# One core of Trainium2: the meta tokens' attention of a hybrid decoder, taken out of the pairs' pipeline and done for eight heads at once

## The chip, the core and the metric

The kernel runs on one core of one Trainium2 chip. The metric is the device time of one execution in microseconds (us). Before the change it is 1934.89 us, the median of three runs (1934.46 to 1937.74). The core's engines work on their own instruction queues and meet through semaphores: TensorE (PE for its matmuls, PEld for its weight loads), VectorE (DVE), ScalarE (ACT), GpSimd (POOL), and SyncE (SP), whose queue issues the DMAs.

## The reference, cut to what matters

The reference is a trunk of two layers (DEPTH is 2) over 16 learned meta tokens followed by 1024 positions, 1040 rows of width 1024. Each layer normalizes its input and projects it into the operands of two parallel mixers: sliding-window attention, and an mLSTM with four heads. Both outputs are gated and go through one output projection. The first 16 rows are dropped at the end.

```python
h = rms_norm(x, norm_g)
z = h @ w_in
aq, ak, av, ag, mq, mk, mv, mi, mf, mo, mgate = split(z)
q = partial_rope(rms_norm(aq.reshape(B, L, 16, 64), q_norm_g))
k = partial_rope(rms_norm(ak.reshape(B, L, 2, 64), k_norm_g))
ya = sliding_window_sink_attention(q, k, av, sink) * silu(ag)
...
y = concatenate([ya, ym]) @ w_out
return x + y
```

There are 16 query heads and 2 key heads, eight query heads to each key head. A query sees itself and the 127 positions before it, and also all 16 meta tokens; each head has one more logit, its sink, that takes part in the softmax but has no value. A meta token's own query therefore sees only the meta tokens up to itself, and the sink: a 16 by 16 lower triangle and one column. That part of the attention is needed in layer 0 alone, since the meta rows of layer 1's output are dropped.

## The kernel before, in words

All matmuls are in full float32 accuracy by splitting operands into a high and a low float32r part and adding the products. The rows are cut into nine tiles (`TT`): tile 0 has the 16 meta rows, tiles 1 to 8 have 128 rows each. Layer by layer the kernel runs four stages: keys and values for all tiles (`kv_tasks`) and the first group of queries; the attention; the mLSTM; the output projection.

**The attention stage** goes through eight pairs of heads, `j` = 0 to 7 (pairs 0 to 3 use key head 0, pairs 4 to 7 key head 1, `kv`). For each pair it goes through blocks of queries `b` (`att_tasks`). In layer 0 these are nine, b = 0 to 8, block 0 being the meta tokens; in layer 1 `first_q` is 1 and there are eight. A block passes four steps:

- `s1` (L680): the scores of both heads into a score tile S, four matmuls (L692). S is two PSUM banks wide, one bank for each head, and there are two such tiles, used in turn. Then the mask (L704 to L711), the maximum (L715), the exponential (L718), the reciprocal of the sum (L720) and the scaling (L723). Some blocks' S also takes turned queries of a coming pair in its free columns 384 to 511 (`q_turn`, L633, and `q_take`, L639 to L642: the `visits`), and in layer 0 block 6's takes the meta queries of the next pair (`q_meta_turn`, L646).
- `s2`, two blocks later: the probabilities are transposed into the one bank T (L738, L741), and split into high and low parts by ACT and DVE (L745, L746, L748, L749); POOL makes a masked copy, OW (L756).
- `s3`, three blocks later: the first product with the values into the one bank O (L766).
- `s4`, behind s3: the other products (L778) into O. ACT takes half of O out (L781), DVE adds the other half (L783), POOL multiplies the result into the gate tile G (L785), and SP stores finished chunks of G to `spool` in DRAM (L789).

For block 0 the forms are small: 16 queries and 16 keys in s1, one 16x16 transpose in s2, nothing in s3, two products of 16 columns in s4.

**What sets the order.** Beside the attention, projections run: while pair j passes, the gates (even j, `g_tasks`, 22 parts for two pairs) or the next queries (odd j below 7, `q_tasks`, 24 parts in layer 1 and 25 in layer 0, where the meta tile is a part of its own) or the mLSTM's first values (j = 7, 25 parts) are computed in small parts (L234 and, for the meta tile, L218). A q group is taken out of its bank by ACT (L580, L581) and DVE (L584) at its last part. `weave` spreads the items of the pair's steps evenly over the parts:

```python
for i, f in enumerate(fg):
    f()
    upto = (i + 1) * len(bg) // len(fg)
    for g in bg[done:upto]:
        g()
```

`fg` are the parts and `bg` the items: four for each step (s1 of one block, s2 of an earlier one, s3 and s4 of one earlier still), so 36 a pair in layer 0 and 32 in layer 1. In this stage PE's instructions keep exactly this order (`pin`). The order on ACT, DVE and POOL, and PE's in the mLSTM, is set by a scheduler that runs through the program with a simulated time; `high_priority` puts some instructions ahead. Weights come by DMA (L161) and are split by ACT (L167) and POOL (L168) into a ring of buffers; their loads hang on places in the list of parts, their splits on `s2` of certain blocks. The stage ends when the last block has passed s4, and the mLSTM follows with the rest of the projections (L194).

Of the kernel before, what the change touches and what calls it, by code (L numbers as in the profile page):

```python
# [12 lines left out]
F32R = mybir.dt.float32r  # L13
# [10 lines left out]
NEG = -1e30  # L24
# [12 lines left out]
WHEN = {0: (3, 4, 5, 6), 3: (2, 3, 4, 5), 4: (3, 4, 6, 7)}  # L37
FIRST = ((0, 0), (0, 1), (1, 0))


def _tables():
# [10 lines left out]
    cst = np.zeros((128, 166), f)  # L52
    cst[:, 0:128] = np.eye(128, dtype=f)
    cst[:, 128:164] = -0.5
    for r in range(64):
        cst[r, 164 + r // 16 % 2] = 1.0
    return {
# [7 lines left out]
def build(ctx, tc, I, O):  # L65
# [307 lines left out]
    for l in range(DEPTH):  # L373
# [5 lines left out]
        AV = unit(F32R)[:, 0:896].rearrange("p (t c) -> p t c", t=7)  # L379
        DV = unit(F32R)[:, 0:896].rearrange("p (t c) -> p t c", t=7)  # L380
# [3 lines left out]
        KT = unit()[:, :].rearrange("p (a c) -> p a c", a=8)  # L384
        SS = []
# [87 lines left out]
        def kv_tasks():  # L473
# [13 lines left out]
            if l == 0:  # L487
# [4 lines left out]
                sy.dma_start(cst, I["cst"])  # L492
# [25 lines left out]
            for i in range(4):  # L518
                ve.tensor_scalar(VM[:, i // 2, i % 2, :], ident, 0.0, None, ALU.mult)
            for i, t in enumerate(ts):  # L520
# [123 lines left out]
        def q_meta_turn(j, ps):  # L644
            c0 = 128 * (j % 2)
            pin(pe.transpose(ps, A[j]["q"]["XM"][:, c0:c0 + 128], ident[:16, :16]))  # L646

        def q_meta(j, ps):

            q_meta_turn(j, ps)  # L650
            q_put(q_unit(j, 0)[:, 1024:1056], ps, 16)

        def g_tasks(j, wgf, co, st):
            def chunk_parts(c):
# [4 lines left out]
                def finish(ps):  # L659
                    if c == 0:  # L660
                        st["G"] = unit()
                    th = t384(e - a)
                    sc.activation(th, ps[:, :e - a], AF.Tanh, scale=0.5)
                    ve.scalar_tensor_tensor(st["G"][:, a:e], th, 1.0, ps[:, :e - a], ALU.add, ALU.mult)
                return projT_parts(wgf, co, a, e - a, finish)
# [11 lines left out]
        def att_tasks(j, st):  # L677
# [3 lines left out]
            def s1(b):  # L681
# [4 lines left out]
                k0, kn, o = (0, 16, 128) if b == 0 else (0, 144, 128) if b == 1 else (16 + (b - 2) * 144, 272, 0)  # L686
                for h in range(2):
                    U = st["Q", b > 4]
                    i = (b - 1) % 4
                    lq = U[:, 1024 + 16 * h:1040 + 16 * h] if b == 0 else U[:, 512 * h + 128 * i:512 * h + 128 * i + 128]  # L690
# [3 lines left out]
                meta = b == 6 and j < 7 and first_q == 0  # L694
                if meta:
                    q_meta_turn(j + 1, S[:, 0, 384:400])
# [6 lines left out]
                if b == 0:  # L703
                    ve.memset(band[:p], NEG)  # L704
                    mk = mask[:p, 128:144].bitcast(U32).rearrange("p (a c) -> p a c", a=1).to_broadcast([p, 2, 16])
                    ve.copy_predicated(cols(S, 130, 510, 16)[:p], mk,
                                       neg[:p].rearrange("p (a c) -> p a c", a=1).to_broadcast([p, 2, 16]))
                else:
                    if b == 1:
                        ve.memset(cols(S, 2, 510, 128), NEG)  # L710
                    ve.copy_predicated(band, mask.bitcast(U32).rearrange("p (h c) -> p h c", h=2),  # L711
                                       cols(S, 146, 366, 128))
# [13 lines left out]
                if meta:  # L726
                    q_put(q_unit(j + 1, 0)[:, 1024:1056], S[:, 0, 384:400], 16)
                live[b] = P

            def s2(b):  # L730
# [3 lines left out]
                HL = OW = None  # L734
# [4 lines left out]
                if b > 0:  # L739
                    for h in range(2):  # L740
                        pin(pe.transpose(X[:, 128 * h:128 * h + 128], P[:, 1 + 160 * h:129 + 160 * h], ident))  # L741
                with tc.high_priority(offset=EARLY):
                    if b > 0:
                        HL = p512(F32R)
                        sc.activation(HL[:, 0:256], X[:, 0:256], AF.Copy)  # L745
                    taken = sc.activation(pm[0:32, 0:p], tm, AF.Copy).ins  # L746
                    if b > 0:
# [619 lines left out]
```

## Time and profile before

| what | value |
|---|---|
| median of three runs | 1934.89 us (1934.46 to 1937.74) |
| the profiled execution | 1933.47 us |
| its span, first to last instruction | 1931.7 us |
| granted TensorE clock | 1.000 |
| busy over the span: PE, PEld, DVE, ACT, POOL | 98%, 93%, 54%, 55%, 51% |

The profile's page is of one execution. "Idle" of an engine is time with no instruction running on it; the waits view says which instruction came after such a time and which one, as far as semaphores tell, let it go. A row of the timeline has the start in us from the beginning of the span, the length in us, the engine, the line, the operation, what it writes and reads, the shape, and a count where like instructions are merged. A row of the windows view has the stretch, its length, then the busy us of each engine with its number of instructions in brackets, the granted clock, the DMA engines' busy share and GB/s. Matmuls are pipelined: a new one starts before the last has ended, so a group's share of TensorE's time is read from the start of one group to the start of the next.

### The profile page before, as it was taken

To read this page: it belongs to the slowest core of one execution; us is meant where nothing else is said; L and a number is where in the kernel's file an instruction comes from. 1 tells how busy PE (TensorE), PEld (TensorE's weight loads), DVE (VectorE), ACT (ScalarE), POOL (GpSimd) and SP (SyncE) were. 2 spreads that over 40 slices of the span, in tenths; PEclk is the share of its full clock that TensorE was granted. 3 is DMA by queue.
4 is the path that set the end of the run, shared out by engine and by line. 5 is a ranking of instruction groups with operands and counts; after the bars stand their busy time and mean duration, and the time that the engine had idled before them with its cause. 6 is when DMAs were issued, how large, how long until landed. Compare 5 with 4: busy or idle time off the path is not lost.

```text
span 1931.7 us, 36274 instructions
## 1 busy us (share of the span) xinstructions
PE 1902.6 (98%) x12827; PEld 1796.5 (93%) x12827; DVE 1051.2 (54%) x2914; ACT 1065.0 (55%) x3193; POOL 988.7 (51%) x1278
## 2 busy tenths in 40 slices
PE   8999999999999999999999999999999999999999
PEld 7999999999999999977789999999999999998887
DVE  7666766667354453542545667666573635437211
ACT  6577777746454554643334778776564545446221
POOL 3665756346545454564325467564465543647332
PEclk9999999999999999999999999999999999999999
DMA  4111111121222121554541111112122121216543
GB/s 155 32 45 40 38 44 43 45 65 41 64 54 59 43 62 50 154 170 159 176 134 36 44 48 38 49 48 60 40 59 64 47 71 41 62 59 195 167 148 125
DMA packets 150839, 148.28 MB, mean 77 GB/s; under 512 B 15081, under 2 KB 123921, under 8 KB 150658
## 3 DMA queue, kind: packets, MB, share of 16 engines
q1 hardware_dynamic: 150658, 145.97, 25.8%
q8 instruction: 101, 1.65, 0.4%
q14 instruction: 80, 0.66, 0.1%
HBM read 122.58 MB, written 23.29 MB: 76 GB/s over the span
## 4 chain that ended last, share of the span: by engine, by line
PE 82%; DVE 5%; ACT 3%; DMA 3%; POOL 3%; issue 2%; SPq 0%; ACTq 0%; POOLq 0%; DVEq 0%
PE pj L194 32%; PE pj L234 19%; PE pss L1260 6%; PE pj L1260 5%; PE po L1260 4%; PE S L692 3%; PE O L778 3%; PE po L957 2%; PE pss L957 2%; PE O L766 2%; PE T L741 1%; DMA raw<-in_w_out_dram 1%; DVE t L903 1%; PE pt L957 1%; PE pj L218 1%
## 5 line engine op out<-in xcount | busy, mean ns | idle before, releaser
L194 PE MATMUL pj<-H,RING 128*128 128x384 f32 (+2 forms) x3312 | 559.3, 322 | 0.0
L194 PEld LDWEIGHTS pj<-H,RING 128*128 128x128 f32 x3312 | 521.5, 188 | 2.3 <-issue 0.2
L168 POOL TENSOR_TENSOR RING<-raw,RING 128x512 fp32r<-128x512 f32 (+1 forms) x192 | 256.8, 1343 | 107.3 <-ACT RING L167 100.3
L234 PE MATMUL pj<-RING,H 128*128 128x256 f32 (+1 forms) x1920 | 268.8, 286 | 0.0
L234 PEld LDWEIGHTS pj<-RING,H 128*128 128x128 f32 x1920 | 242.2, 189 | 0.5
L234 PE MATMUL pj<-H,RING 128*128 128x384 f32 (+2 forms) x1296 | 239.7, 325 | 0.0
L186 POOL TENSOR_TENSOR RING<-raw,RING 128x512 fp32r<-128x512 f32 x96 | 126.1, 1320 | 172.8 <-ACT RING L185 159.7
L194 PE MATMUL pj<-RING,H 128*128 128x256 f32 x1536 | 209.6, 287 | 4.0 <-DVE w1k L202 2.1
L234 PEld LDWEIGHTS pj<-H,RING 128*128 128x128 f32 x1296 | 200.9, 188 | 0.1
L194 PEld LDWEIGHTS pj<-RING,H 128*128 128x128 f32 x1536 | 193.7, 191 | 6.5 <-DVE w1k L202 2.5
L185 ACT ACTIVATE RING<-raw 128x512 fp32r<-128x512 f32 x128 | 80.6, 631 | 174.8 <-DMA raw<-in_w_out_dram 155.4
L167 ACT ACTIVATE RING<-raw 128x512 fp32r<-128x512 f32 (+1 forms) x196 | 122.2, 625 | 47.0 <-DMA raw<-in_w_in_dram 35.2
L970 POOL TENSOR_TENSOR p<-u,p 128x258 fp32r<-128x258 f32 x64 | 49.5, 774 | 172.9 <-ACT p L969 164.9
L718 ACT ACTIVATE t<-S,mx 128x145 f32<-128x145 f32 (+1 forms) x272 | 99.4, 368 | 43.9 <-DVE mx L715 35.3
L785 POOL TENSOR_TENSOR u<-u,w1k 128x128 f32<-128x128 f32 (+1 forms) x136 | 61.9, 455 | 118.0 <-DVE w1k L783 102.2
L1260 PE MATMUL pss<-RING,H 128*128 128x512 f32 x384 | 120.5, 394 | 0.0
L756 POOL TENSOR_SCALAR_AFFINE_SELECT p<-p 128x512 fp32r<-128x512 f32 x112 | 71.4, 637 | 86.7 <-DVE p L748 85.7
L1260 PE MATMUL pj<-RING,H 128*128 128x512 f32 x352 | 110.3, 395 | 0.0
L903 DVE SCALAR_TENSOR_TENSOR t<-u,cw,t 128x384 f32<-128x384 f32 (+1 forms) x144 | 107.6, 747 | 2.0
L723 ACT ACTIVATE t<-t,mx 128x144 f32<-128x144 f32 (+1 forms) x272 | 97.7, 407 | 7.1 <-DVE mx L720 6.5
L926 DVE SCALAR_TENSOR_TENSOR t<-t,pj 128x384 f32<-128x384 f32 (+2 forms) x48 | 24.5, 511 | 124.9 <-ACT t L925 124.9
L1260 PE MATMUL po<-RING,H 128*128 128x512 f32 x288 | 91.3, 398 | 0.0
(347 smaller groups left out, 3841.3 us busy)
## 6 DMA issues: line engine op xcount, KB each, us to landing
raw<-in_w_out_dram SPq DMA_DIRECT2D x128, 256.0 KB, 2.8
raw<-in_w_in_dram SPq DMA_DIRECT2D x100, 256.0 KB, 2.8
raw<-in_w_in_dram SPq DMA_DIRECT2D x192, 128.0 KB, 2.3
spool<-u SPq DMA_DIRECT2D x56, 192.0 KB, 1.9
p<-x SPq DMA_DIRECT2D x24, 256.0 KB, 4.2
t<-spool SPq DMA_DIRECT2D x30, 192.0 KB, 3.6
p<-spool SPq DMA_DIRECT2D x26, 192.0 KB, 3.6
u<-em SPq DMA_DIRECT2D x8, 576.0 KB, 6.6
```

The source lines that it names most:

```text
L167: sc.activation(hi, raw[:, :, 0:o], AF.Copy)
L168: eng.tensor_tensor(lo, raw[:, :, 0:o], hi, op=ALU.subtract)
L185: sc.activation(hi, raw, AF.Copy)
L186: (ve if i > 8 and i % 2 else gp).tensor_tensor(lo, raw, hi, op=ALU.subtract)
L194: last = pin(pe.matmul(out, a, b, start=(i == 0), stop=(i == n - 1)))
L234: pin(pe.matmul(out(), x, y, start=(k + i == 0), stop=(k == n - 1 and i == 2)))
L718: sc.activation(P[:p, 145 * h:145 * h + 145], S[:p, h, 1 + 127 * h:146 + 127 * h], AF.Exp, bias=mx[:p, 0, h:h + 1], accum_out=mx[:p, 1, h: ...
L723: sc.activation(Pn, Pn, AF.Copy, scale=mx[:p, 2, h:h + 1])
L756: gp.affine_select(OW, HL, [[0, 4], [1, 128]], ALU.is_ge, 0.0, base=0, channel_multiplier=-1)
L903: ve.scalar_tensor_tensor(z, RAW[:, t0 + i:t0 + i + n], wcol(i), z, ALU.mult, ALU.add)
L957: pin(f(*a, **k))
L1260: pin(pe.matmul(ps[:p, :], a, b, start=(i + n == 0), stop=(i == 15 and n == len(terms) - 1)))
```

## The change

Block 0 goes out of the pairs' pipeline. Every pair has eight blocks in both layers, b = 1 to 8, and 32 items in its weave. In layer 0 the meta queries are handled so instead:

- After each of the four query groups, the turned meta queries of four heads are split and put into one stationary operand `QM`, which has eight heads by 16 meta queries, 128 columns, for each key head. It lies in free columns of the unit that holds `AV`. The first group is put there before the attention, the others in block 6 of pairs 1, 3 and 5 (before: one pair at a time, eight times).
- Two blocks carry the rest (`MRIDE`): block 4 of pair 3 for key head 0, block 4 of pair 7 for key head 1. Their s1 has two more matmuls, into columns 384 to 399 of S's first bank: 128 rows (eight heads by 16 queries) by 16 meta keys. `meta_probs` masks, adds the sink column and takes the softmax. Their s2 has one more transpose, into T's free columns, and its split into `pmm`, which lies in free columns of the unit that holds `DV`. Their s4 has one more product of 128 columns, into O's columns 256 to 383, and `meta_out` takes it out of the bank, adds the halves, multiplies with the gates and stores the 16 meta rows of four pairs to `spool`.
- The gates' first 16 columns are copied by POOL into `GM` (free space of VR's first tile) as each gate chunk 0 is done; nine small DMAs in pair 0 bring the triangle and the sinks into free space of KR's first tile.
- The store of a pair's first chunk begins at column 16 in both layers.

```diff
+MRIDE = ((3, 4), (7, 4))
...
+        def q_meta_turn(m, ps):
+            for i in range(2):
+                pin(pe.transpose(ps[:, i], QQ[m]["XM"][:, 128 * i:128 * i + 128], ident[:16, :16]))
...
+        def meta_probs(S, kv):
+
+            X = S[:, 0, 384:401]
+            one = lambda x: x.rearrange("p (a c) -> p a c", a=1)
+            ve.copy_predicated(one(X[:, 0:16]), one(mcst[:, 32:48].bitcast(U32)), one(neg).to_broadcast([128, 1, 16]))
+            ve.tensor_copy(X[:, 16:17], mcst[:, 48 + kv:49 + kv])
+            P, mx = mcst[:, 0:17], mcst[:, 20:23]
+            ve.tensor_reduce(mx[:, 0:1], X, axis=mybir.AxisListType.X, op=ALU.max, negate=True)
+            sc.activation(P, X, AF.Exp, bias=mx[:, 0:1], accum_out=mx[:, 1:2])
+            ve.reciprocal(mx[:, 2:3], mx[:, 1:2])
+            sc.activation(P[:, 0:16], P[:, 0:16], AF.Copy, scale=mx[:, 2:3])
+            return P
+
+        def meta_out(O, kv):
+
+            O = O[:, 256:384]
+            up, y = w1k(), w1k()
+            sc.activation(up[0:64, 0:128], O[64:128], AF.Copy)
...
+            for h in range(2):
+                ve.tensor_tensor(y4[64 * h:64 * h + 64], o[:, h], u[:, h], op=ALU.add)
+            gp.tensor_tensor(y4, y4, GM[:, 4 * kv:4 * kv + 4], op=ALU.mult)
+            sy.dma_start(spool[4 * kv:4 * kv + 4, :, 0:16].rearrange("j p t -> p j t"), y4)
...
+                    if a == 0:
+                        gp.tensor_copy(GM[:, j], st["G"][:, 0:16])
...
-                meta = b == 6 and j < 7 and first_q == 0
+                meta = b == 6 and j in (1, 3, 5) and not last
                 if meta:
-                    q_meta_turn(j + 1, S[:, 0, 384:400])
+                    q_meta_turn((j + 1) // 2, S[:, :, 384:400])
+                if (j, b) in MRIDE and not last:
+                    for i in range(2):
+                        pin(pe.matmul(S[:, 0, 384:400], QMF[:, 128 * kv:128 * kv + 128], Ks[i][:, 0:16], start=(i == 0), stop=(i == 1)))
...
-                if b == 0:
-                    ve.memset(band[:p], NEG)
...
-                if b > 0:
...
+                    if pmeta is not None:
+                        sc.activation(pmm[0:16], tmm, AF.Copy)
+                        ve.tensor_tensor(pmm[32:48], tmm, pmm[0:16], op=ALU.subtract)
...
+                if ride:
+                    pin(pe.matmul(mo[:, 256:384], VM[:, kv, 0, :], pmm, start=True, stop=True))
...
+                    if ride:
+                        meta_out(mo, kv)
...
-            return [(b, s1, s2, s3, s4) for b in range(first_q, 9)]
+            return [(b, s1, s2, s3, s4) for b in range(1, 9)]
...
+        def meta_consts():
+
+            sy.dma_start(mcst[:, 32:48], I["cst"][:, 166:182])
+            s0 = I["attn_sink"][l]
+            for h in range(8):
+                sy.dma_start(mcst[16 * h:16 * h + 16, 48:50],
+                             bass.AP(tensor=s0.tensor, offset=s0.offset + h, ap=[[0, 16], [8, 2]]))
```

91 lines of the change are left out of this document (53 added, 38 removed).

## The prediction

> **What bounds the kernel now.** I read the page first, then the two attention stretches in the windows view, then the waits of the weight loads in each, then the timeline of the longest wait.
>
> ```profile
> PE 1902.6 (98%) x12827; PEld 1796.5 (93%) x12827; DVE 1051.2 (54%) x2914; ACT 1065.0 (55%) x3193; POOL 988.7 (51%) x1278
> ...
> PE 82%; DVE 5%; ACT 3%; DMA 3%; POOL 3%; issue 2%; SPq 0%; ACTq 0%; POOLq 0%; DVEq 0%
> ```
>
> The first line is busy time by engine, the second the chain that ended last. TensorE bounds the kernel and no other engine is over 55%. So time can come only from matmuls that go and from TensorE's waits.
>
> ```profile
> core 0: us, PE busy (x) PEld busy (x) DVE busy (x) ACT busy (x) POOL busy (x), PEclk, DMA share, GB/s
> 79.70:403.30 323.60, 315.77 (x2417) 307.86 (x2415) 219.23 (x686) 237.87 (x830) 181.17 (x283) 1.00 0.15 43
> 403.30:800.00 396.70, 394.48 (x2737) 387.12 (x2736) 204.60 (x612) 207.13 (x603) 204.02 (x258) 1.00 0.20 54
> ...
> 1059.60:1357.30 297.70, 297.52 (x2309) 295.20 (x2308) 201.83 (x610) 216.33 (x744) 172.03 (x254) 1.00 0.17 47
> ```
>
> The first and the last row are the attention stages of layer 0 and layer 1, each from its first score matmul to its last output product; the middle row is layer 0's mLSTM, for later. Layer 1 already runs without the meta queries: eight steps for a pair, against nine in layer 0. That makes it the nearest row to the changed stage. Layer 0's stage is 25.9 us longer. It leaves PE idle for 7.8 us (323.60 less 315.77), where layer 1 leaves 0.2, and the weight loads for 15.7 us, where layer 1 leaves 2.5. The next view, the weight loads' waits in layer 0's stretch, gives them names:
>
> ```profile
> engine line waited for: us in total, times, longest us
> PEld O L766 <- ACT ptm L746: 6.3, 6, 1.7
> PEld O L766 <- ACT t L723: 2.4, 3, 0.9
> PEld T L738 <- issue: 1.1, 5, 0.3
> PEld O L766 <- ACT t L663: 0.9, 3, 0.4
> PEld O L766 <- ACT u L444: 0.5, 1, 0.5
> ...
> PEld O L766 <- issue: 0.4, 1, 0.4
> PEld T L738 <- ACT t L723: 0.3, 1, 0.3
> ```
>
> 10.5 us are lost before L766, the first product into bank O, and 1.4 us before L738: 11.9 together. Layer 1's stretch has 0.9:
>
> ```profile
> PEld T L738 <- ACT u L639: 0.5, 1, 0.5
> PEld O L766 <- issue: 0.4, 2, 0.2
> ```
>
> The longest of layer 0's waits, in the timeline:
>
> ```profile
> 229.35 0.45 PE L778 MATMUL O<-p,u 128*128 128x256 f32 x2
> ...
> 230.85 0.60 ACT L580 ACTIVATE u<-pj 128x512 f32<-128x512 f32 x1
> ...
> 231.35 0.59 ACT L581 ACTIVATE pj<-pj 128x512 f32<-128x512 f32 x1
> ...
> 231.97 0.38 ACT L781 ACTIVATE w1k<-O 64x256 f32<-64x256 f32 x1
> ...
> 232.94 0.57 DVE L783 TENSOR_TENSOR w1k<-O,w1k 64x128 f32<-64x128 f32 x2
> ...
> 233.63 0.30 PEld L766 LDWEIGHTS O<-p,u 128*128 128x128 f32 x2 [1.66 <-ACT ptm L746]
> ```
>
> The releaser that the view names is only the one inferred. O has one buffer, and L766 starts right after L783, its last reader, ends at 233.51. O was full at 229.80, but its evacuation L781 stood in ACT's queue behind L580 and L581, the evacuations of the projection's group.
>
> How much TensorE work hides that queue is set by the weave. A pair's steps, four items each, are laid evenly over the pair's projection parts: 36 items over 22 parts (even pairs) or 25 (odd ones) in layer 0. Counting floor((i+1) x 36 / parts) through, between a step's s4 and the next step's s3 stand one part at the fewest and two as a rule. In layer 1, with 32 items over 22 or 24, it is two at the fewest, and three everywhere in the odd pairs 1, 3 and 5.
>
> **The change, part by part.** First the matmuls, by their starts in the timeline:
>
> ```profile
> 79.72 0.25 PE L692 MATMUL S<-u 128*16 128x16 f32 x4
> 79.83 2.35 PE L234 MATMUL pj<-H,RING 128*128 128x384 f32 x12
> ...
> 86.22 0.19 PE L738 MATMUL T<-cst,t 16*32 16x16 f32 x1
> 86.33 0.77 PE L692 MATMUL S<-u 128*128 128x272 f32 x4
> ...
> 88.22 0.27 PE L738 MATMUL T<-cst,t 128*32 128x128 f32 x1
> 88.33 0.38 PE L741 MATMUL T<-cst,t 128*128 128x128 f32 x2
> ...
> 89.60 0.29 PE L778 MATMUL O<-ptm,VM 128*128 128x16 f32 x2
> 89.74 1.30 PE L234 MATMUL pj<-H,RING 128*128 128x384 f32 x6
> ...
> 102.88 0.33 PE L778 MATMUL O<-ptm,VM 128*128 128x128 f32 x2
> 103.05 0.46 PE L778 MATMUL O<-p,u 128*128 128x256 f32 x2
> ```
>
> - Removed, eight times: block 0's scores (79.72 to 79.83, 0.11), its transpose (86.22 to 86.33, 0.11) and its two products (89.60 to 89.74, 0.14): 8 x 0.36 = 2.9 us.
> - Added, twice: two score matmuls with full weights and 16 moving columns (as L778's pair, 0.14), one transpose (as 88.22 to 88.33, 0.11), one 128-column product (half of 102.88 to 103.05, 0.09): 2 x 0.34 = 0.7 us. The turns of the meta queries stay eight transposes. Net: 2.2 us less, all on the bounding engine.
>
> **The waits.** Eight steps instead of nine put 32 items over 22 or 25 parts. By the same count, two parts at the fewest now stand between s4 and s3, so the one-part steps go. The even pairs get exactly layer 1's weave, and I give them layer 1's waits, 0.9 us in all for the stage. The odd pairs do not: the meta tile's projection remains as a 25th part, so that five of their eight steps keep two parts where layer 1 has three, and by the count the projection groups' ends (parts 7, 13, 19 and 25) each fall on an s4, the case of the timeline above. In pairs 1, 3 and 5 two such steps each have only two parts to cover it. Each may cost from nothing (layer 1) to 1.66 (the row above), 0 to 10 us for six; block 0's small operations no longer stand in ACT's and DVE's queues there, and I take 0.5 each, 3.0.
>
> The riding adds a wait of its own. In s4 the meta product goes into O's columns 256 to 383, and O comes free only after one more ACT copy and two more DVE adds, by L781 (0.38) and L783 (0.57) at most 0.95. The next block's L766 is queued behind that. Two rides: 0 to 1.9, I take 0.8, nearer the lower end since the new operands are half as wide or less. The Trainium skill ("PSUM — Partial Sum Buffer", PSUM bank collisions raise a hardware error) says that two engines on one bank collide even at disjoint columns, so a bank is guarded whole. By that rule spare columns are not free: L766 would wait for the meta readers in full, this term would be 1.9 and the result 1926.6. No run shown here has such a rider.
>
> Waits after: 0.9 + 3.0 + 0.8 = 4.7, against 11.9: 7.2 us less.
>
> **What I cost at nothing.** The rows, from the timeline and from SP's waits in this stretch:
>
> ```profile
> 92.73 0.22 POOL L785 TENSOR_TENSOR u<-u,w1k 128x16 f32<-128x16 f32 x1 [0.97 <-DVE w1k L783]
> ...
> 235.57 0.34 SPq L789 DMA_DIRECT2D spool<-u  x1
> ```
>
> ```profile
> SPq L161 <- POOL RING L168: 171.9, 34, 32.5
> ```
>
> Eight copies of the gate's first 16 columns join POOL's queue and eight such L785 (0.22) leave it. A copy waits for DVE's gate product, with the mask of OW (L756) and the weights' L168 behind it; no wait of TensorE in the views above is on POOL. If that cover went, 8 x 0.2 would show. Nine small DMAs (mask and sinks) join SP's queue in pair 0, about 9 x 0.34 = 3.1 us of issue; behind them are weight loads, which wait 171.9 us in this stretch for POOL to free the ring (34 times, 5 us each), and that hides them. Uncovered, one weight group would come up to 3.1 us late. The two stores of the meta rows wait on SP for POOL as L789's do. S has two buffers and a step is 4.3 us (323.6 over 72 steps and three of drain), so the meta softmax, two steps ahead of its transpose, is covered. ACT and DVE shed more (block 0's ops, eight times) than they gain (twice). All these: 0.
>
> **Sum.** 2.2 + 7.2 = 9.4 us. The profiled execution took 1933.47 us (span 1931.7), 1.4 under the median 1934.89. It becomes 1924.1, and the median **1925.5 us**.
>
> **The rivals.**
> - *All of the weight loads' excess idle goes.* With two parts everywhere O is always free in time, the riders' readers too are done early, and the small losses that no wait names vanish with the stalls. 15.7 less 2.5 is 13.2, with the 2.2: 15.4, 1919.5. For it: layer 1's even pairs. Against it: the 25th part. 0.15. (The Trainium skill, "Perfetto Trace Analysis", Identifying the Most-Contended Engine, measures TensorE's headroom by the weight loads' busy share and not the matmuls'. The windows agree in so far as the loads' row leaves 15.7 us idle where the matmuls' leaves 7.8.)
> - *The odd pairs keep all theirs.* Six steps at 1.05 us (the mean of L766's first row, 6.3 over 6): 6.3 in place of 3.0, so 6.1 gained, 1928.8. For it: L580 and L581 stay. 0.12.
> - *The waits do not come from the spacing.* If ACT's crowding alone holds O, and the step count does not matter, only the matmuls go: 2.2, 1932.7. This is also the case of a change that does not do what it says to the waits. For it: the quoted wait stands in an odd pair, where two parts and not one lay between. Against it: layer 1, with ACT as busy (216.33 of 297.70, 73%, against layer 0's 74%), has none. 0.13.
> - *The order outside the attention is worse.* The scheduler orders the unpinned mLSTM stretches anew after any edit. In layer 0's, 9.6 of 396.7 us of the weight loads are idle (2.4%). Were both layers' stretches as idle as layer 0's attention now is (15.7 of 323.6, 4.9%), that would be 2 x 2.5% x 396.7 = 19.8 us lost: 10.4 slower, 1945.3. It decides from 9.4 + 3.9 = 13.3 us, 1.7% of both stretches. Against it: none of their operations are edited. 0.05.
>
> **How the numbers follow.** The forecast has 0.55. Two kernels are told apart here from about 0.2%, 3.9 us, so faster means below 1931.0: the forecast and the first two rivals, 0.82. Same: 0.13. Slower: 0.05. The range goes from the first rival's end, 1919.0, to 1931.0, past the second rival (the odd pairs' steps a little worse than 1.1 and the riders at 1.9); it leaves out 0.18.
>
> **What would show it.** In the changed profile: L692, L738 and L778 without 16-column forms but for the two riders; the attention stage of layer 0 about 314 us long instead of 323.6; its weight-load waits at L766 from 10.5 to about 4, those that remain in pairs 1, 3 and 5 after L580/L581 and in the step after a ride; layer 1 and the mLSTM stretches unchanged within 1 us. The forecast is wrong if L766's waits stay near 10 with eight steps, if the even pairs keep theirs, or if the gain of the stage turns up as idle time behind it.

## The result, and the profile after

The changed kernel takes 1918.1 us, the median of four runs (1917.71 to 1919.48), against 1935.17 (1934.46 to 1937.74) for the kernel before beside it: a ratio of 0.9914 (95% interval 0.9901 to 0.9927), so 14 to 19 us less. The forecast was 1925.5 with 1919.0 as the low end of its range. The sign and the place were right; the gain is 1.8 times the one forecast, and the result lies 0.9 under the range. The profiled execution of the changed kernel is the slowest of its four: 1919.48 us, span 1917.8, 13.9 under the span before. One of the ten executions of the last kernel in the table further down took 2294.84 us at a granted clock of 0.754, and medians and ratios are of the others.

The busy line and the chain of the page:

```profile
PE 1894.3 (99%) x12779; PEld 1792.5 (93%) x12779; DVE 1039.3 (54%) x2865; ACT 1051.8 (55%) x3131; POOL 988.3 (52%) x1280
...
PE 87%; DVE 4%; issue 3%; POOL 2%; DMA 2%; ACT 1%; SPq 0%; POOLq 0%; ACTq 0%; DVEq 0%
```

TensorE is still the bound and holds more of the chain, 87% where it was 82%; ACT went from 3% to 1%. The windows view, with the stages that the prediction read (layer 0's attention, layer 0's mLSTM, layer 1's attention), shows where:

```profile
core 0: us, PE busy (x) PEld busy (x) DVE busy (x) ACT busy (x) POOL busy (x), PEclk, DMA share, GB/s
80.00:386.90 306.90, 306.42 (x2369) 303.22 (x2368) 207.79 (x636) 223.94 (x768) 182.63 (x285) 1.00 0.16 46
386.90:784.50 397.60, 394.43 (x2736) 386.93 (x2735) 204.91 (x611) 207.07 (x603) 203.93 (x258) 1.00 0.20 54
1046.30:1344.10 297.80, 297.59 (x2310) 295.26 (x2308) 201.96 (x610) 216.80 (x744) 172.55 (x254) 1.00 0.17 47
```

The edited stage went from 323.60 to 306.90, 16.7 us less, where "about 314" was forecast. The weight loads' idle time in it fell from 15.7 to 3.7 (306.90 less 303.22), and their busy time by another 4.6 (307.86 to 303.22). The mLSTM is 0.9 longer and layer 1's attention 0.1. (The Trainium skill, "Perfetto Trace Analysis", Identifying the Most-Contended Engine, has TensorE's headroom read from the loads' busy share. The trace agrees in so far as the loads' row gave up 12.1 us of idle time, the matmuls' row only 7.3, from 7.8 to 0.5, of a gain of 16.7.) All waits of the weight loads in the new stage:

```profile
PEld T L774 <- issue: 0.5, 1, 0.5
PEld T L774 <- ACT u L647: 0.5, 1, 0.5
PEld O L805 <- issue: 0.4, 2, 0.2
PEld S L654 <- issue: 0.3, 2, 0.2
```

L774 and L805 are the old L738 and L766. What was 11.9 us there is 1.4. No wait is on POOL or a weight, so the nine small DMAs, the copies into `GM` and the stores cost nothing that shows.

Two gains have to be kept apart: 16.7 in the stage and 13.9 in the whole span. From here on the stage is measured from its first gate matmul, a little ahead of the first score matmul, to its last product into O: 326.60 before, 309.90 after. In a second execution of the same changed kernel it is 309.90 again. Between the two kernels' profiles the rest differs by 2.8: the start-up +0.3, the mLSTM +1.0, the output projection with layer 1's keys and values +2.1, layer 1's attention 0.0, the rest -0.6. The largest, the output projection's stretch, is 256.0 before and 258.1 after.

Two more things moved with the number of steps, and neither the change's description nor the prediction names them. The first visit for a pair (turned queries that are put into S and taken out by ACT and DVE) stood in block 8 of the preceding pair, and now it stands in block 7. And the weights' splits hang on `s2` of the next higher block, block 2 where it was block 1, and so on.

### The profile page after: what moved, and what is told of

It reads as the page before. It is cut to its first block, busy times and chain, and to the rows that moved or that the text cites. A ratio compares the mean times of both kernels' runs of the same rounds, so it can differ in the third digit from the quotient of the medians.

```text
span 1917.8 us, 36063 instructions
## 1 busy us (share of the span) xinstructions
PE 1894.3 (99%) x12779; PEld 1792.5 (93%) x12779; DVE 1039.3 (54%) x2865; ACT 1051.8 (55%) x3131; POOL 988.3 (52%) x1280
## 4 chain that ended last, share of the span: by engine, by line
PE 87%; DVE 4%; issue 3%; POOL 2%; DMA 2%; ACT 1%; SPq 0%; POOLq 0%; ACTq 0%; DVEq 0%
PE pj L196 32%; PE pj L236 20%; PE pss L1320 7%; PE pj L1320 6%; PE po L1320 5%; PE S L730 3%; PE O L817 3%; PE po L1002 2%; PE pss L1002 2%; PE O L805 2%; PE T L776 1%; PE pt L1002 1%; PE pj L220 1%; DVE t L948 1%; PE T L774 1%
## 5 line engine op out<-in xcount | busy, mean ns | idle before, releaser
L169 ACT ACTIVATE RING<-raw 128x512 fp32r<-128x512 f32 (+1 forms) x196 | 122.4, 626 | 48.7 <-DMA raw<-in_w_in_dram 38.4
L752 ACT ACTIVATE t<-S,mx 128x145 f32<-128x145 f32 x256 | 93.6, 368 | 36.5 <-DVE mx L749 32.0
L830 POOL TENSOR_TENSOR u<-u,w1k 128x128 f32<-128x128 f32 x128 | 60.4, 472 | 92.3 <-DVE w1k L826 85.0
L757 ACT ACTIVATE t<-t,mx 128x144 f32<-128x144 f32 x256 | 92.0, 407 | 4.4 <-DVE mx L754 3.8
L783 ACT ACTIVATE p<-T 128x256 fp32r<-128x256 f32 x128 | 49.1, 384 | 80.2 <-PE T L776 73.5
## 6 DMA issues: line engine op xcount, KB each, us to landing
raw<-in_w_out_dram SPq DMA_DIRECT2D x128, 256.0 KB, 2.8
raw<-in_w_in_dram SPq DMA_DIRECT2D x100, 256.0 KB, 2.8
p<-x SPq DMA_DIRECT2D x24, 256.0 KB, 4.1
```

Of the source, the lines that this page charges most:

```text
L169: sc.activation(hi, raw[:, :, 0:o], AF.Copy)
L752: sc.activation(P[:p, 145 * h:145 * h + 145], S[:p, h, 1 + 127 * h:146 + 127 * h], AF.Exp, bias=mx[:p, 0, h:h + 1], accum_out=mx[:p, 1, h: ...
L757: sc.activation(Pn, Pn, AF.Copy, scale=mx[:p, 2, h:h + 1])
```

## The experiments

The theory after the result was that spacing does it: with nine steps over the same projection parts O is wanted again before its queue has run, with eight it isn't. The rivals: block 0's small matmuls cost TensorE far more than their 2.9 us; or block 0's operations on ACT and DVE were what made the queues long. Each experiment is meant to give back to the changed kernel one thing that the change took away. Its measure is the stage in one profiled execution. It repeated to 0.1 us in the one kernel that was profiled twice, while the start-up alone goes from 74.8 to 81.3 over the runs, so the medians don't follow the stages step by step. The granted clock in the stage was 1.00 in all but two of these profiles, which are named below. Each ratio is to executions of the kernel before that ran beside that kernel. Kernels called "without riders" leave the meta tokens' attention of layer 0 out (the two riding blocks' matmuls, softmax and product); those on which they are built do the same.

| kernel | stage, us | median, us | ratio to before (95%) |
|---|---|---|---|
| before | 326.6 | 1935.17 | 1 |
| after | 309.9 | 1918.1 | 0.9914 (0.9901 to 0.9927) |
| after, once more | 309.9 | 1916.81 | 0.9912 (0.9896 to 0.9927) |
| 24 parts in odd pairs | 310.3 | 1918.51 | 0.9922 (0.9910 to 0.9935) |
| ninth step, empty | 317.9 | 1926.43 | 0.9964 (0.9951 to 0.9976) |
| ... two of them | 323.4 | 1931.69 | 0.9989 (0.9980 to 0.9998) |
| ninth step, small matmuls | 323.5 | 1930.42 | 0.9979 (0.9970 to 0.9988) |
| eight steps, small operations in block 1's banks | 326.4 | 1932.11 | 0.9995 (0.9985 to 1.0005) |
| eight steps, small operations on scratch | 313.4 | 1923.26 | 0.9945 (0.9932 to 0.9959) |
| without riders | 308.6 | 1916.55 | 0.9913 (0.9899 to 0.9926) |
| ... ninth step, empty | 313.0 | 1921.22 | 0.9926 (0.9911 to 0.9940) |
| ... with small matmuls | 318.2 | 1923.97 | 0.9941 (0.9926 to 0.9955) |
| ... with operations on scratch too | 320.0 | 1930.78 | 0.9971 (0.9959 to 0.9984) |
| ... these reading O | 320.0 | 1929.91 (one run) | |
| ... reading T | 320.7 | 1930.0 (one run) | |
| ... reading S, with a turn of its own | 322.9 | 1937.89 (one run) | |
| ... reading all three | 323.0 | 1930.27 | 0.9980 (0.9969 to 0.9989) |

**The changed kernel once more**, unedited.

> The changed kernel once more, unedited, for a second profile of it: its median is 17.1 us under the kernel before, but its first profile's span only 13.9 us under (1917.8 against 1931.7), with layer 0's attention 16.7 us shorter and 2 to 3 us lost again behind it. If those 2 to 3 us belong to the change, the second profile shows them in the same places (layer 0's output projection and layer 1's keys and values, 261.8 us against 259.6, and the mLSTM, 397.6 against 396.7). If they are scatter of one execution, some of them are gone and the span comes to about 1916.

```profile
74.80:384.70 309.90, 309.42 (x2393) 306.24 (x2392) 208.50 (x637) 224.47 (x770) 184.73 (x291) 1.00 0.16 45
```

The stage is the same to 0.1 us, the span 1914.5, so 17.2 under before's. The mLSTM's 1.0 us (397.5 here, as before) and the start-up are scatter; the output projection stays at 258.5, 2.5 over before's. Its granted clock is 0.99 here, but 1.00 in the first profile, which is as long; so the clock isn't the whole reason. Over all the profiles that stretch goes from 256.0 (before) to 261.4, with its operations unedited. The reason was not looked for.

**An empty ninth step**: the old spacing, nothing in it. The other two edits keep the visits and the weights' splits at the changed kernel's blocks (not at the old kernel's).

```diff
-            return [(b, s1, s2, s3, s4) for b in range(1, 9)]
+            skip = lambda b: None
+            return [(0, skip, skip, skip, skip)] * (not last) + [(b, s1, s2, s3, s4) for b in range(1, 9)]
...
-        visits = {j * ns + 4 * g + i - 2: (j, g, i)
+        visits = {j * 8 + 4 * g + i - 2: (j, g, i)
...
-                splits[steps[j * ns + i - 2][:2]] = nxt.split
+                splits[steps[j * ns + i - 2 + ns - 8][:2]] = nxt.split
```

> The changed kernel with four empty items put back for each pair of layer 0, where block 0's stood: nine steps and 36 items in the weave again, but no work in the ninth. Theory of the spacing (the recorded one): the waits at the first product into O come from steps with too few projection parts between s4 and the next s3; they come back at nearly their old size, 8 to 10 us in the weight loads' waits, and the time rises to about 1927. Rival, the queues: block 0's own small operations on ACT and DVE and its own turn of O made the waits; then at most 1 us comes back, 1918 to 1919. A share of both would lie near 5 us, since about half of the old waits stood behind steps shorter than any that the changed kernel has.

```profile
75.10:393.00 317.90, 312.08 (x2393) 307.37 (x2392) 210.16 (x637) 225.77 (x770) 183.55 (x291) 1.00 0.16 44
```

8.0 us come back with not one instruction added. Its largest waits, and the first one in the timeline:

```profile
PEld O L805 <- issue: 3.0, 4, 2.3
PEld O L805 <- ACT ptm L784: 1.8, 3, 1.4
PEld O L805 <- ACT t L757: 1.4, 1, 1.4
```

```profile
220.29 1.58 DVE L451 TENSOR_TENSOR u<-u 64x576 fp32r<-64x576 f32 x2
220.63 0.26 ACT L681 ACTIVATE w1k<-O 64x128 f32<-64x128 f32 x1
222.27 0.45 DVE L685 TENSOR_TENSOR w1k<-O,w1k 64x64 f32<-64x64 f32 x2
222.83 0.30 PEld L805 LDWEIGHTS O<-p,u 128*128 128x128 f32 x2 [2.34 <-issue]
...
222.86 0.47 PE L805 MATMUL O<-p,u 128*128 128x256 f32 x2 [2.13 <-DVE w1k L685]
```

This wait is a rider's: L685, the last reader of its product, stands on DVE behind a 1.58 us subtraction of the next keys (L451, `k_stacks`), and the product's bank is wanted again. In the changed kernel L685 runs ahead of L451. The 1.4 behind L757 is the other rider's. The old kernel had no riders, so 8.0 is too much for the spacing: the riders had to go from the test.

**Two empty steps**: the same line with `* (2 * (not last))`.

> The changed kernel with eight empty items for each pair of layer 0 in place of four: 40 items over 22 or 25 parts, work unchanged. The mean number of parts between s4 and the next s3 falls from 2.06 (32 items over 22) and 1.83 (36) to 1.65. Theory of the spacing: the waits grow with each cut; after 7.9 us for the first four items, 15 us or more in the stage for eight, about 325 us, and a time of about 1933. If the four items' 7.9 us came from where they happened to put single steps of pairs 3 and 4 (half of its waits stood there), eight items give no more than about 8, 318 us.

```profile
75.30:398.70 323.40, 313.52 (x2392) 308.50 (x2391) 209.71 (x637) 224.44 (x770) 184.58 (x291) 0.99 0.16 43
```

```profile
PEld S L730 <- ACT u L672: 3.1, 1, 3.1
```

The stage loses 0, 8.0 and 13.5 us with none, one and two empty steps. But the waits at the first product into O didn't grow with the second one (7.4 with one, 7.2 with two). A wait at S came, for the softmax of a rider (L672 is `meta_probs`), and the granted clock in the stage was 0.99. So this run doesn't show a price of spacing that grows.

**A ninth step with the small matmuls**, on constant operands: four score matmuls of 16 columns, one transpose, two products of 16 columns. No other engine reads them.

```diff
+            z16 = VM[:, kv, 0, 0:16]
...
+                        pin(pe.matmul(S[:16, h, 130 - 2 * h:146 - 2 * h], z16, Ks[i][:, 0:16], start=(i == 0), stop=(i == 1)))
...
+                pin(pe.transpose(bank("T")[0:32, 256:272], ident[:16, 0:32], ident[:16, :16]))
...
+                    pin(pe.matmul(O[:, 16 * h:16 * h + 16], VM[:, kv, h, :], z16, start=True, stop=True))
...
+            return [(0, z1, z2, skip, z4)] * (not last) + [(b, s1, s2, s3, s4) for b in range(1, 9)]
```

> The same nine steps, and in the ninth step's items block 0's seven small TensorE instructions a pair (four score matmuls of 16 columns, one 16x32 transpose, two products of 16 columns) on constant operands, with nobody reading the results. Over the kernel with empty items: by the recorded price (group start to group start) 8 x 0.36 = 2.9 us more; by the fall of the weight loads' busy time in the stage (307.9 to 303.2, with 0.7 for the riders added) about 5 us more. It also takes its turns of S, T and O, so that a wait for a free bank can come on top.

```profile
75.40:398.90 323.50, 317.62 (x2448) 310.89 (x2447) 209.91 (x637) 226.04 (x770) 183.78 (x291) 1.00 0.16 43
```

5.6 us over the empty step, where the prediction had 2.9 for the same matmuls. The timeline of the kernel before shows what its price left out:

```profile
83.70 1.03 PE L234 MATMUL pj<-H,RING 128*128 128x384 f32 x5
84.56 0.67 PE L692 MATMUL S<-u 128*128 128x272 f32 x4
...
85.94 0.34 PE L234 MATMUL pj<-H,RING 128*128 128x384 f32 x1
```

Five gate matmuls and the step to the scores behind them take 0.86, 0.17 each. But from the start at 85.94 to the small transpose at 86.22 it is 0.28: the 0.11 that the prediction read from the transpose to the next matmul is half of what the transpose takes, 0.21 or 0.22 in all. From the matmul ahead to the one behind, less the usual distance, eight transposes are 1.68 us in this run, the scores 0.84 and the products 1.13: 3.7.

That is still too little, because the matmul right behind a group is slow to let the next one start. Here are the second starts behind the scores, the transpose and the products that the prediction showed (the first were at 79.83, 86.33 and 89.74):

```profile
80.09 0.52 PE L234 MATMUL pj<-H,RING 128*128 128x384 f32 x2
86.56 0.41 PE L692 MATMUL S<-u 128*128 128x272 f32 x2
90.00 0.51 PE L234 MATMUL pj<-H,RING 128*128 128x384 f32 x2
```

These steps are 0.26, 0.23 and 0.26, where 0.17 is usual for 384 columns and 0.13 for 272 (the four scores from 84.56 to the next matmul at 85.07). Over all groups of the run with small matmuls they add 2.2 us: 5.8 from the matmul ahead to the second one behind, against 5.6 measured. No turn of a bank is needed to explain it: the waits at the first product into O are 7.4 us with the empty step and 7.6 with the small matmuls.

**Block 0's operations on ACT and DVE**, with eight steps: first reading S, T and O beside block 1's own readers, then the same forms on scratch.

```diff
+                if b == 1 and not last:
+                    z_probs(S, mx)
...
+                        sc.activation(zp[0:32, 0:16], tm[:, 0:16], AF.Copy)
+                        ve.tensor_tensor(zp[32:64, 0:16], tm[:, 0:16], zp[0:32, 0:16], op=ALU.subtract)
...
+                        sc.activation(zu[0:64, 0:32], O[64:128, 0:32], AF.Copy)
```

> The changed kernel with eight steps, and block 0's work on DVE, ACT and POOL put into block 1's steps (memset, masked copy, maximum, two exponentials, reciprocal, two scalings, and the small evacuations of T and O), eight times, without its TensorE work and without the ninth step. Theory of the spacing: TensorE has the same parts between its steps and hides it, at most 1 us more, 1918 to 1919. Rival, the queues: a large part of the old waits comes back, 4 to 8 us, at the O products of blocks 1 to 3.

> Block 0's DVE, ACT and POOL operations in block 1's steps again, eight steps, but now all on scratch in SBUF, so that they lengthen the queues without holding S, T or O or a work buffer (the run before held T and S longer and so made waits of its own at S and T). The stage is measured from the first gate matmul to the last product into O: 309.8 us in the changed kernel, 326.5 before, 317.7 with empty items, 323.4 with empty items and small matmuls. Theory of the spacing: at least two parts stand between s4 and s3 and cover the queues; at most 1 us more, 310 to 311. Rival, the queues: the rest of the stage's difference, 326.5 less 323.4 with the riders' 0.8 added, is theirs also with eight steps: 313 to 314 or more.

```profile
75.20:401.60 326.40, 315.20 (x2393) 310.97 (x2392) 219.18 (x693) 238.53 (x834) 186.27 (x299) 0.98 0.16 43
```

```profile
PEld S L747 <- ACT t L729: 5.0, 3, 2.1
```

The first is a poor test: the old kernel never had two blocks' readers on one turn of a bank, and waits of 5.0 us at S, that it did not have, are the edit's own. The granted clock in its stage was 0.98 besides, so part of its 16.5 us is the clock's. On scratch the stage is 3.5 longer than the changed kernel's, and in the range of the rival, not of the spacing. Its waits in pair 0 add to 3.5, where the old kernel's add to 1.1. So it says that such operations aren't free, and not what they cost at their old places.

**24 parts in pairs 1, 3 and 5**: the meta tile's part joined to the next one.

```diff
+            if j in (1, 3, 5) and len(fg) == 25:
+                fg = [lambda a=fg[0], b=fg[1]: (a(), b())] + fg[2:]
```

> The changed kernel with the meta tile's projection in pairs 1, 3 and 5 joined to the next part: 24 parts, three parts between s4 and s3 throughout as in layer 1. The recorded step held that the 25th part costs 3.0 us in these pairs; the changed kernel's profile shows two waits of 0.2 us there. So at most 0.5 us less in the stage, 309.3 to 309.8, and a time that can't be told from the changed kernel's. If it comes out faster by more, the 25th part costs in ways that the waits do not show.

```profile
75.30:385.60 310.30, 309.65 (x2393) 306.52 (x2392) 209.82 (x638) 225.24 (x770) 184.15 (x291) 1.00 0.16 45
```

Nothing is gained. The two waits that remain at L805 (0.2 each, at 132.5 and 280.1) were all that the 25th part could cost.

**Without riders.** Removed are their score matmuls, `meta_probs`, the transpose, `pmm`, the product and `meta_out`.

```diff
-                    for i in range(2):
-                        pin(pe.matmul(S[:, 0, 384:400], QMF[:, 128 * kv:128 * kv + 128], Ks[i][:, 0:16], start=(i == 0), stop=(i == 1)))
...
-                    pin(pe.matmul(mo[:, 256:384], VM[:, kv, 0, :], pmm, start=True, stop=True))
...
-                        meta_out(mo, kv)
+                        sy.dma_start(spool[4 * kv:4 * kv + 4, :, 0:16].rearrange("j p t -> p j t"), GM[:, 4 * kv:4 * kv + 4])
```

> The changed kernel without the riders' work: block 4 of pairs 3 and 7 carry no meta scores, softmax, transpose, product or evacuation, and the store takes the copied gates as they are; so the meta tokens' attention is left out of layer 0. The recorded step priced the riders' matmuls at 0.7 and the longer hold of O at 0.8 (0 to 1.9). The changed profile shows no wait at O behind a ride; then the stage gets shorter by the matmuls alone, 0.7 to 0.9, to about 309. With the hold it would be 1.5 or more, below 308.3.

```profile
75.10:383.70 308.60, 308.42 (x2384) 305.43 (x2383) 204.78 (x623) 222.27 (x760) 184.50 (x289) 1.00 0.16 45
```

Two rides cost 1.3 us in all, 0.8 of it matmuls. The other 0.5 is one wait in the changed kernel, behind the second ride, at T and not at O:

```profile
363.09 0.28 DVE L789 TENSOR_TENSOR u<-T,u 16x128 fp32r<-16x128 f32 x1
...
363.49 0.09 PEld L774 LDWEIGHTS T<-cst,t 128*32 128x32 f32 x1 [0.49 <-issue]
363.52 0.27 PE L774 MATMUL T<-cst,t 128*32 128x128 f32 x1 [0.30 <-DVE u L789]
```

L789 is the rider's last reader of T, and the next transpose waits for it; the run without riders has no such wait. From here the old kernel was built up again step by step.

**An empty ninth step, then its small matmuls**, without riders (the edits are those above).

> Four empty items a pair again, but without the riders (no meta attention in layer 0, as in the run without riders, whose stage was 308.6 us). The first run with empty items has its longest waits, 2.3 and 1.4 us, behind the riders' evacuation of O, so part of its 8.0 us was not the old kernel's. If the spacing alone made the old waits, the stage is 8 us longer than 308.6, about 316.6. If the riders made 3.7 of them, about 4 us longer, 312 to 313, and the spacing explains less than half of the old 10.5 us of waits at O.

> The ninth step with block 0's seven small TensorE instructions, without the riders. Over the run above: 2.9 us by the recorded price; 3.8 by what the timeline of the run with riders shows from the matmul ahead of each group to the one behind it, less the usual distance of those two; 5.6 as the run with riders gave. The last would mean that the ninth turns of S, T and O cost as well.

```profile
74.90:387.90 313.00, 310.74 (x2385) 306.47 (x2384) 207.92 (x623) 224.04 (x760) 183.38 (x289) 1.00 0.16 45
```

```profile
74.80:393.00 318.20, 316.23 (x2440) 310.03 (x2440) 208.00 (x623) 224.30 (x760) 183.47 (x289) 1.00 0.16 44
```

The spacing alone is 4.4 us (313.0 less 308.6), not 8.0: the waits at the first product into O go from 0.4 to 3.9. The matmuls are 5.2 more, close to the 5.6 with riders, and these waits do not grow with them (3.2).

**The operations of block 0 on scratch, and then on the banks**, in the ninth step of the last kernel: on none, on O alone, on T alone, on S alone, on all three. With S, block 0 also takes a turn of S's two tiles, and the last edit then puts the first visit for a pair back into block 8.

```diff
-                    sc.activation(zf[0:64, 660:692], zf[64:128, 700:732], AF.Copy)
+                    sc.activation(zf[0:64, 660:692], O[64:128, 0:32], AF.Copy)
...
+            def z_probs(S):
+                ve.memset(cols(S, 2, 654, 128)[:16], NEG)
...
                 S = SS[blk[0] % 2]
+                blk[0] += 1
...
-        visits = {j * 8 + 4 * g + i - 2: (j, g, i)
+        visits = {j * ns + 4 * g + i + ns - 10: (j, g, i)
```

> As the run above, and block 0's DVE, ACT and POOL operations in the ninth step's items too, on scratch in SBUF: the old kernel's block 0 in everything but that its operations do not wait for one another across engines (nobody reads S, T and O). The old stage was 326.6. If spacing, matmuls and queues together are the whole of it, this stage comes to 324 to 327. If it stays below 322, the rest is the chain itself: O, S and T held by block 0 until its own evacuation.

> The ninth step with matmuls and queue operations (stage 320.0 us, no riders), now with block 0's evacuation reading O as in the old kernel: O is held by block 0's turn until ACT and DVE have read it. Old stage 326.6, so 6.6 us are open. If the ninth turn of O is their place, the stage comes to 324 to 326.5, with new waits at the first product into O of block 1. If not, it stays within 1 us of 320.

> The same with only T held: ACT and DVE read block 0's transposed probabilities from T. Block 1's transposes come a whole step later, so I expect nothing, 320 to 320.5. If T's ninth turn is the place of the open 6.6 us, waits at the first transpose (now 2 us) grow and the stage comes to 324 or more.

> The same with only S: block 0 takes a turn of the two score tiles of its own and its softmax reads it, and the queries' visits stand as in the old kernel. S is turned over nine times a pair, and block 0's softmax waits for its scores and holds DVE's and ACT's queues meanwhile. If this is the place of the open 6.6 us, the stage comes to 324 or more; if S is covered by its two tiles, 320 to 321.

> All three held: the old kernel's block 0 complete but for the path from its softmax to its products. The stage should come back to 325 to 326.6 and the time to about 1933 to 1935. If it stays below 323, what is left is the chain from step to step itself (a softmax that waits for its scores, a transpose for its softmax) or the order that the scheduler makes of it, which these runs don't separate.

The stages on scratch, on S alone, and on all three:

```profile
81.20:401.20 320.00, 316.52 (x2440) 309.93 (x2440) 214.10 (x652) 232.78 (x799) 182.54 (x289) 1.00 0.16 44
```

```profile
81.30:404.20 322.90, 317.66 (x2440) 310.46 (x2439) 216.16 (x659) 236.62 (x810) 182.00 (x286) 1.00 0.16 43
```

```profile
77.00:400.00 323.00, 317.94 (x2440) 310.40 (x2439) 219.73 (x679) 237.81 (x824) 184.79 (x297) 1.00 0.16 43
```

On scratch the operations cost 1.8. But 1.6 of it is one wait, in pair 0, behind a weight split on ACT (L169):

```profile
PEld O L793 <- ACT RING L169: 1.6, 1, 1.6
```

The old kernel has no wait over 0.4 in pair 0, and with O held this one is 0.5. The scheduler orders ACT, DVE and POOL anew after every edit, so this can be an accident of the order and not a price of the operations. For the same reason little can be read into O's 0.0 and T's 0.7. S adds 2.9, and all three 3.0. No wait at S appears with it; the waits at the first product into O go from 4.6 on scratch to 7.2. In the last kernel's waits and timeline the first product into O is L793, its evacuation L810 and L812:

```profile
PEld O L793 <- ACT ptm L775: 4.2, 5, 1.7
PEld O L793 <- issue: 1.5, 5, 0.4
```

```profile
228.14 0.37 ACT L647 ACTIVATE u<-S 64x256 fp32r<-64x256 f32 x1
...
228.52 0.38 ACT L648 ACTIVATE u<-S 64x256 fp32r<-64x256 f32 x1
...
228.93 0.60 ACT L588 ACTIVATE u<-pj 128x512 f32<-128x512 f32 x1
...
229.42 0.59 ACT L589 ACTIVATE pj<-pj 128x512 f32<-128x512 f32 x1
...
230.04 0.38 ACT L810 ACTIVATE w1k<-O 64x256 f32<-64x256 f32 x1
230.10 0.27 DVE L825 MEMSET S<- 16x256 f32 x1
...
231.01 0.57 DVE L812 TENSOR_TENSOR w1k<-O,w1k 64x128 f32<-64x128 f32 x2
...
231.70 0.30 PEld L793 LDWEIGHTS O<-p,u 128*128 128x128 f32 x2 [1.71 <-ACT ptm L775]
```

This is the wait of 1.66 us that the prediction quoted, rebuilt: 1.71 with the same ACT operations in front. The prediction showed the pair of query evacuations (here L588 and L589). Ahead of them stand two more, L647 and L648, which are a visit's; in the kernel before they are L639 at 230.07 and L640 at 230.45. On scratch, with that visit in block 7, they are not there, and the same step has no wait:

```profile
232.40 0.57 ACT L588 ACTIVATE u<-pj 128x512 f32<-128x512 f32 x1
...
233.47 0.38 ACT L810 ACTIVATE w1k<-O 64x256 f32<-64x256 f32 x1
...
234.77 0.30 PEld L793 LDWEIGHTS O<-p,u 128*128 128x128 f32 x2
```

By these rows the visit's two copies are some 0.8 of the 1.71 (an estimate from L647's start to L588's), and block 0's first operation on S (L825, 0.27) stands in DVE's queue as well. So the 2.9 is the price of S's turn and of the visit in block 8 together. No run has one without the other.

**The ledger.** The stage, built up from the run without riders:

| step | stage, us | adds |
|---|---|---|
| eight steps, no riders | 308.6 | |
| ninth step, empty | 313.0 | 4.4 |
| its small matmuls | 318.2 | 5.2 |
| its ACT, DVE and POOL operations, on scratch | 320.0 | 1.8, nearly all one wait |
| these on S, T and O, with S's turn and the visit in block 8 | 323.0 | 3.0 |
| the kernel before | 326.6 | 3.6, open |

That is 18.0, and with the riders' 1.3 the stage's 16.7. The sizes hold in this order of building; the terms are not independent, as the spacing's 8.0 with riders and 4.4 without shows. The first two are shown by what they add and where; the next two, 4.8 together, only as a sum. The 3.6 are what is left between a block 0 of constants and the real one: its chain from step to step, the scheduler's order around it, the weights' splits at the old blocks, and single turns of the meta queries in seven blocks instead of double ones in three. They were not told apart.

## Why the prediction was wrong in size

**The bound and the place: right.** Nothing but TensorE's own work and waits moved; L766's waits were the largest item, layer 1's attention (already eight steps) foretold the changed stage's waits, and it did not change itself.

**Where the 7.3 us between the stage's 16.7 and the forecast 9.4 lie.** The waits named at O and T fell by 10.5 and not by 7.2, which is 3.3. The other 4.0 are in TensorE's own steps and in small losses that no wait names, where the prediction had 2.2 us of matmuls.

**"8 x 0.36 = 2.9 us": mis-sized.** It is 3.7 from the matmul ahead to the one behind, 5.8 to the second one behind, and 5.2 to 5.6 in the stage. The step that failed is reading a group from its own start to the next start: what a small group does to the matmul ahead of it, and to the step behind the next one, was left out. A part was in the sum under another name: the 1.4 us of waits before L738 are idle time before the weight loads of six of the eight small transposes, and the small transposes of constants in the run with small matmuls have 1.5 of it too. The added 0.7 was right: 0.8.

**"I take 0.5 each, 3.0" for the odd pairs: failed.** Without the 25th part nothing is gained, and the waits at L805 are 0.4 in all. In the changed kernel two parts between s4 and s3 are enough, and this term was 2.6 us too much.

**"Two rides: 0 to 1.9, I take 0.8": nothing at O, 0.5 at T.** The hold of O is there, and hidden; the hold of T, which the prediction didn't price, cost the 0.5 shown above. The changed kernel's first ride:

```profile
217.49 0.22 PE L821 MATMUL O<-u,VM 128*128 128x128 f32 x1
...
218.16 0.58 DVE L826 TENSOR_TENSOR w1k<-O,w1k 64x128 f32<-64x128 f32 x2 [0.16 <-ACT w1k L824]
218.84 0.28 ACT L681 ACTIVATE w1k<-O 64x128 f32<-64x128 f32 x1 [0.70 <-DVE w1k L826]
219.48 0.45 DVE L685 TENSOR_TENSOR w1k<-O,w1k 64x64 f32<-64x64 f32 x2
220.10 0.31 PEld L805 LDWEIGHTS O<-p,u 128*128 128x128 f32 x2
```

O's last reader ends at 219.93 where without the ride it would be 218.74, and L805 comes at 220.10 with no wait. With nine steps the two holds cost 2.3 and 1.4. There the first hold is longer too, to 222.72, since L685 stands behind L451. L805, which writes columns 0 to 255, waits until L685 has read columns 256 to 383. (That is the rule of the Trainium skill, "PSUM — Partial Sum Buffer", PSUM bank collisions raise a hardware error, that a bank is guarded whole; the 2.13 us wait agrees with it, but the 1926.6 forecast by it did not come, since in the changed kernel L685 ends before L805 is due.)

**"ACT and DVE shed more (block 0's ops, eight times) than they gain (twice). All these: 0": the gain was in the sum, under the wrong cause.** All of the old waits that went were laid on the spacing. In the runs block 0's operations, its turns of the banks and the visit in block 8 add 4.8 us that the spacing doesn't.

**The spacing** is a cause, but its 4.4 us are less than the 7.2 laid on it. Of the old kernel's 10.5 us of waits at the first product into O it brings back 3.9. With all of block 0's operations, and the visit at its old block, they are 7.5; the rest is open. The quoted wait of 1.66 is 0.3 with the spacing alone.

**The rivals.** The first, that all of the loads' excess idle time goes, came nearest: 12.1 of its 13.2 us went, and its 1919.5 is 1.4 over the result; it shares the matmuls' mis-sized term. The third, that the waits do not come from the spacing, is refuted as put: the empty step costs 4.4. Its mechanism, ACT's and DVE's crowding, is nonetheless a part, and set against the spacing as an either-or it was not added to it. The sign that the prediction gave for it, that the quoted wait stands where two parts and not one lay between, was the right one. The second and the fourth did not happen.

**Where gain was given back.** The two profiles' other stages took 2.8 of the 16.7 us, of which the second profile keeps the 2.5 in the output projection. By the medians, 17.1 us apart, nothing is given back on the whole.

## What to carry to other kernels

When small work is taken off a bound engine, price it from the instruction ahead of it to the second one behind it, and then look at what its operations do on the idle engines: where a single bank is evacuated by an engine that is busy 74% of the stage, what stands ahead in its queue delays that evacuation, and the bound engine pays. A weave, its queues and the bank's turns give one wait together; take away each alone in an experiment before a gain is laid to one of them. An experiment on a changed kernel can be upset by what the change added: rebuild the old conditions without it, and check that everything else stands where it stood.

## What the runs showed of the hardware that was not expected

- A lone transpose of 16 rows behind matmuls of 384 columns takes 0.21 us of TensorE, not the 0.11 to the next start: the step into it is 0.28 where one between large matmuls is 0.17. And the matmul right behind a small group takes longer to its next start, 0.26 against 0.17 (384 columns) or 0.23 against 0.13 (272).
- The attention stage's length repeats to 0.1 us over two executions of one program, while the start-up goes from 74.8 to 81.3 us over the runs. The granted clock in the two longest start-ups, 81.2 and 81.3, was 0.94, in the shortest 1.00.
- Work around S can show as waits at another bank: with block 0's turn of S and the visit in block 8, 2.9 us more in the stage, the waits at O went from 4.6 to 7.2 us and none at S appeared.
